# Down groups 1 to 3 of a hybrid block: three of four weight-block sums are accumulated in SBUF instead of in device memory

## The chip, the cores and the metric

The kernel runs on one core of one Trainium2 chip. The metric is the device time of one execution in microseconds (us); a kernel's time is the median of several runs. Where a profile is quoted it is one execution taken by the hardware profiler, with times counted from the start of its span.

## The reference

One layer of a hybrid block on 512 tokens of width 1024, all in float32: a gated delta rule branch and a retention branch, each gated and projected, added to the input after a norm, and then a feed-forward part. Only the last part bears on the change:

```python
hn = rmsnorm(x, n_mlp_pre)
ff = jnp.square(jax.nn.relu(hn @ w_up)) @ w_down      # 1024 -> 4096 -> 1024
return x + rmsnorm(ff, n_mlp_post)
```

## The kernel before, in words

**Feed-forward.** The 4096 hidden features are worked in four groups of 1024 (`for grp in range(4)`, L1991). In each group `feature_major` multiplies with `w_up`, the square of the relu is taken, and `seven_down` (L1885) multiplies 512 tokens x 1024 features with the 1024 x 1024 block of `w_down` that belongs to the group. That block is cut into quarters of 512 x 512, written 11, 12, 21, 22, and the product is made of seven products of quarters instead of eight (a Strassen-Winograd scheme). Three take a plain quarter of the weights (11, 12, and the one called s4, which is 22 of the columns); four take a sum of quarters. In the order of the code for groups 1 to 3: products 11, 12, s2, s1, s3, s4, 22. Group 4 (`grp == 3`) takes another order and is not touched.

**Weights.** Every quarter arrives in two halves of 128 partitions x 1024 numbers (512 KB). Each half is loaded by SyncE's queue into a `raw` tile, then split for TensorE into a rounded part `whi` (ScalarE, L148) and a rest `wlo` (VectorE, L149). `whi` and `wlo` have three buffers each, `raw` has two in each of two pools. TensorE then makes 12 matmuls with each half, 24 with each quarter (`token_product`, L303 to L325, L317).

**Block sums.** `BlockSums` (L155) makes the four sums of quarters in device memory while earlier stages run: it copies a quarter to a tensor `sums` (`copy`, L169, SyncE's queue) and adds further quarters or sums to it by accumulating transfers (`add_block`, L135, GpSimd's queue). `summed` then loads the halves as any other weight (`raw`, L183, L197). Of the four tensors of a group, `t[2]` holds 12+22, `t[1]` 11+12+22, `t[3]` all four, `t[0]` 11+12.

**Order.** A job (one half to copy or to add) is handed out in `pace` (L113), which every weight load calls: when the planned TensorE time `spent` has passed `queued`, one job is placed behind that load, and `queued` moves on by `JOB_US` = 8.5 us (L29, L121). Jobs not yet handed out when a sum is loaded are all issued at that point (L184 to L187). The order of instructions on each engine is fixed when the program is built, from program order, priorities (`tc.high_priority`) and which buffers come free; an engine issues in that order, and SyncE and GpSimd issue transfers in order too: one that waits holds all behind it.

**Tile `ym`.** The pool `pm` has four buffers of 128 x 1024 numbers under the tag `ym`; before the change they hold `fw` (L1773 and L1959), the weighted rows of the norms around the feed-forward part.

Of the kernel before, what the change touches and what calls it, by code (L numbers as in the profile page):

```python
# [19 lines left out]
P = 128  # L20
# [5 lines left out]
OFF_BA = 6144  # L26
OFF_QB, OFF_KB, OFF_VB, OFF_GB = 6160, 7184, 8208, 10256
OFF_GA, OFF_GBR = 12304, 13328
JOBS_FROM, JOB_US = 70.0, 8.5  # L29
SMALL_US, CONV_US, TOK_US, PK_US, INV_US, DB_US = 10.5, 6.5, 2.5, 2.0, 46, 1.2  # L30
VT_US, KS_US, PX_US, PC_US, GATE_US, FEAT_US, INV_PRIO, CONV_PRIO, SMALL_PRIO, KEY_PRIO, DECAY_US, AHEAD, TR_US, REC_PRIO, OUT_PRIO, SUM_PRIO = 2.5, 2.4, 3.5, 2.4, 11.0, 1.0, 0, 600, 800, 600, 20.0, 700, 2.2, 900, 900, 300
DFF = 4096
# [31 lines left out]
def hybrid_block_kernel(ctx: ExitStack, tc: tile.TileContext, a: dict, out: bass.AP):  # L64
# [68 lines left out]
    def add_block():  # L133
        dst, src, _ = later_adds.pop(0)
        tc.keep_in_program_order(nc.gpsimd.dma_start(dst, src, accum_op=ALU.add))  # L135
# [19 lines left out]
    class BlockSums:  # L155


        def __init__(self, src, c1, c2, tag, full=True):
            def block(kh, c):
                return src[4 * kh * P : 4 * (kh + 1) * P, c : c + 512].rearrange("(k p) c -> p k c", p=P)  # L160

            self.w12, self.first = block(0, c2), [block(0, c1), block(0, c1), block(1, c2), block(1, c1)]
            self.made = (2, 1, 3, 0) if full else (2, 0)
            self.t = {i: dr.tile([P, 4, 512], F32, tag=f"{tag}{i}", name="sums", bufs=1) for i in self.made}
            self.parts = []
            trickle.extend((self, i, k) for i in self.made for k in (0, 2))
# [13 lines left out]
        def weights(self, i, ks):  # L180
            return split_weights(self.raw(i, ks), 1024, 2)

        def raw(self, i, ks):  # L183
            while any(job[0] is self for job in trickle):  # L184
                copy_block()
            while any(dst is t for dst, *_ in later_adds for t in self.parts):
                add_block()  # L187
            return block_raw(self.t[i - 1][:, 2 * ks : 2 * ks + 2, :])

        def first_raw(self, i, ks):  # L190
            return block_raw(self.first[i][:, 2 * ks : 2 * ks + 2, :])

    def block_raw(block):
        n = next(loads)
        pool, tag = raw_pools[n % len(raw_pools)]
        raw = pool.tile([P, 1024], F32, tag=tag, name="raw", bufs=2)
        load = nc.sync.dma_start(raw.rearrange("p (k c) -> p k c", k=2), block)  # L197
        pace(load)
        return raw

    z_sums = BlockSums(w_in, OFF_ZA + 1024, OFF_ZA + 1536, "z")
    ga_sums = BlockSums(w_in, OFF_GA, OFF_GA + 512, "ga", False)
    vg_sums = [BlockSums(w_in, OFF_VB + h * 512, OFF_GB + h * 512, f"vg{h}", False) for h in range(4)]
    gb_sums = BlockSums(w_in, OFF_GBR, OFF_GBR + 512, "gb", False)
    down_sums = [BlockSums(w_down[grp * D : (grp + 1) * D, :], 0, 512, f"dn{grp}") for grp in range(4)]
    for sums in [z_sums, ga_sums] + vg_sums + [gb_sums] + down_sums:
        later_adds.extend((*pair, sums) for pair in sums.adds())

# [19 lines left out]
    def bank(pool):  # L228
        if pool is psx:
            return [psx.tile([P, T], F32, tag="dl", name="dl", bufs=3) for _ in range(2)]  # L230
        return [psm.tile([P, T], F32, tag="mm", name="mm") for _ in range(2)]

    def block_products(src, sums, product):


        def plain(pss, x, kh, c, first):
            for ks in range(2):
                product(pss, x, ks, weights(src, 4 * kh + 2 * ks, 2, c, 512, paced=False), first)

        def summed(pss, x, i, first):  # L240
            for ks in range(2):
                product(pss, x, ks, sums.weights(i, ks), first)

        return plain, summed
# [414 lines left out]
    class Clock:  # L659
# [36 lines left out]
        def ready(self, wait):  # L696
            if isinstance(wait, str):
                return self.events.get(wait, float("inf"))
            return wait
# [1018 lines left out]
    with tc.tile_pool(name="pm", bufs=1) as pm:  # L1718
# [165 lines left out]

        def seven_down(grp, x):  # L1885

            src = w_down[grp * D : (grp + 1) * D, :]
            plain, summed = block_products(src, down_sums[grp], token_product(x))

            def add(th, ch, parts, op=ALU.add, new=False, prio=400):  # L1890
                with tc.high_priority(prio):
                    for t in range(2):
                        dst = facc[:, 2 * th + t, hss[ch]]
                        if not new or grp:
                            nc.vector.tensor_tensor(dst, dst, parts[t], op)
                        elif op is ALU.add:
                            nc.scalar.copy(dst, parts[t])
                        else:
                            nc.scalar.mul(dst, parts[t], -1.0)

            a = bank(psx)
            plain(a, "11", 0, 0, True)
            add(0, 0, a, new=True, prio=100)
            b = bank(psm)
            plain(b, "12", 1, 0, True)
            add(0, 0, b, prio=0)
            c = bank(psm)

            def s1():
                summed(c, "s1", 1, True)  # L1910
                add(1, 1, c, new=True)

            def s2():
                summed(a, "s2", 2, False)
                add(0, 1, a, ALU.subtract, new=True)

            def s3():
                summed(a, "s3", 3, False)
                add(1, 1, a, ALU.subtract)

            for step in (s1, s2) if grp == 3 else (s2, s1, s3):
                step()
            plain(c, "s4", 1, 512, False)
            add(0, 1, c, prio=0)
            if grp < 3:
                summed(a, "22", 4, False)
                add(1, 0, a, new=True)
                return
            for t in range(2):
                rows = Finish(t)  # L1930
                for half in range(2):
                    rows.half(half)
                for half in range(2):
                    rows.store(half)
            ws = {}
            for name, i in (("s3", 3), ("22", 4)):
                kept = pm.tile([P, 8, T], F32R, tag=f"hn{i // 4}", name="keep").rearrange("p k t -> p (k t)")
                for ks in range(2):
                    hi, lo = (kept[:, 1024 * h : 1024 * h + 1024] for h in (2 * ks, 2 * ks + 1))
                    ws[name, ks] = split_weights(down_sums[3].raw(i, ks), 1024, 2, (hi, lo))  # L1940
            rows = [Finish(2 + t) for t in range(2)]
            for name, half, op in (("s3", 1, ALU.subtract), ("22", 0, ALU.add)):
                for t in range(2):
                    for ks in range(2):
                        token_product(x, (t,))(a, name, ks, ws[name, ks], False)
                    dst = facc[:, 2 + t, hss[half]]
                    with tc.high_priority(400):
                        done = nc.vector.tensor_tensor(dst, dst, a[t], op)
                    rows[t].half(half)
            for r in rows:  # L1950
                for half in range(2):
                    with tc.issue_after(done.ins):
                        r.store(half)
# [83 lines left out]
```

## Time and profile before

| what | us |
|---|---|
| median of 3 runs (1326.51 to 1328.75) | 1326.77 |
| the profiled execution, its own time | 1326.62 |
| its span | 1324.8 |
| TensorE busy (PE) | 1308.9 |
| VectorE busy (DVE) | 931.3 |
| ScalarE busy (ACT) | 668.7 |
| GpSimd busy (POOL) | 89.7 |

TensorE is busy in 99% of the span; the chain that ended last runs over PE for 89% of it. The 16 DMA engines moved 223.16 MB. GpSimd issues only the accumulating transfers and a few loads. In the profile, "wlo<-raw,whi" is the split on VectorE, "whi<-raw" that on ScalarE, "sums<-sums" a transfer between two sum tensors, and a mean duration of a matmul (0.39 us) is longer than the distance to the next one, since matmuls are pipelined.

### The profile page before, as it was taken

How to read it: one execution, taken by the hardware profiler on the slowest of the kernel's cores; microseconds unless marked ns; L12 is line 12 of the kernel's file. 1: busy time of each engine (PE TensorE's matmuls, PEld its weight loads, DVE VectorE, ACT ScalarE, POOL GpSimd, SP SyncE). 2: the span in 40 equal slices, each digit the busy share in tenths (PEclk: the TensorE clock that was granted, in tenths of full speed). 3: DMA queues.
4: the chain of work that ended last, by engine and by line, in shares of the span. 5: the costliest groups of instructions: out<-in, count | busy, mean ns of one | idle time of the engine just before them, and what ended most of it. 6: DMA issues, size and time to landing. Idle time of an engine off the chain costs nothing.

```text
span 1324.8 us, 17530 instructions
## 1 busy us (share of the span) xinstructions
PE 1308.9 (99%) x6591; PEld 1085.9 (82%) x6591; DVE 931.3 (70%) x1560; ACT 668.7 (50%) x1168; POOL 89.7 (7%) x95
## 2 busy tenths in 40 slices
PE   9999999999999999999999999999999999999997
PEld 7888787888888878888888888888889888888886
DVE  6889757486666578876567776789685746637478
ACT  5784546455534533544453443465266636355364
POOL 2100100000000001000010000000001000000001
PEclk9999999999999999999999999999999999999999
DMA  5336952476765568887293462545629895859635
GB/s 192 134 112 160 203 132 64 114 181 174 191 161 133 127 178 179 271 253 153 79 260 105 120 214 64 160 157 175 223 82 247 230 256 156 245 154 251 191 119 135
DMA packets 115557, 223.16 MB, mean 168 GB/s; under 512 B 6982, under 2 KB 38896, under 8 KB 114960
## 3 DMA queue, kind: packets, MB, share of 16 engines
q1 hardware_dynamic: 96496, 175.13, 41.3%
q0 software_dynamic: 16944, 40.54, 19.1%
q10 hardware_dynamic: 2032, 6.36, 1.3%
q8 instruction: 52, 0.85, 0.3%
q14 instruction: 33, 0.27, 0.1%
HBM read 216.75 MB, written 72.37 MB: 218 GB/s over the span
## 4 chain that ended last, share of the span: by engine, by line
PE 89%; DVE 6%; ACT 3%; issue 1%; DMA 1%; DVEq 0%; ACTq 0%
PE mm L668 18%; PE mm L317 17%; PE dl L317 11%; PE mm L93 10%; PE mm L95 10%; PE mm L94 10%; PE dl L668 5%; PE tr L397 1%; DVE wlo L149 1%; PE dl L94 1%; PE dl L95 1%; PE dl L93 1%; PE tr L677 1%; PE mm L632 1%; DVE tmp L1061 1%
## 5 line engine op out<-in xcount | busy, mean ns | idle before, releaser
L149 DVE TENSOR_TENSOR wlo<-raw,whi 128x1024 fp32r<-128x1024 f32 x269 | 328.2, 1222 | 204.2 <-ACT whi L148 203.1
L148 ACT CAST whi<-raw 128x1024 fp32r<-128x1024 f32 x269 | 282.6, 1052 | 356.5 <-PE mm L668 71.7
L668 PE MATMUL mm<-actT,whi 128*128 128x512 f32 x448 | 144.5, 403 | 0.0
L317 PE MATMUL mm<-whi,xsum 128*128 128x512 f32 x384 | 120.6, 390 | 0.0
L95 PE MATMUL mm<-hn,wlo 128*128 128x512 f32 (+1 forms) x288 | 105.4, 366 | 0.0
L94 PE MATMUL mm<-hn,whi 128*128 128x512 f32 (+1 forms) x288 | 105.3, 366 | 0.0
L93 PE MATMUL mm<-hn,whi 128*128 128x512 f32 (+1 forms) x288 | 105.3, 366 | 0.0
L668 PEld LDWEIGHTS mm<-actT,whi 128*128 128x128 f32 x448 | 80.6, 188 | 14.8
L668 PE MATMUL mm<-actT,wlo 128*128 128x512 f32 x224 | 87.7, 392 | 0.0
L317 PEld LDWEIGHTS mm<-whi,xsum 128*128 128x128 f32 x384 | 71.8, 188 | 14.9
L317 PE MATMUL mm<-wlo,xsum 128*128 128x512 f32 x192 | 74.8, 390 | 0.0
L317 PE MATMUL dl<-whi,ffq 128*128 128x512 f32 x224 | 71.3, 389 | 0.0
L668 PE MATMUL mm<-whi,og 128*128 128x512 f32 x192 | 62.3, 397 | 0.0
L95 PEld LDWEIGHTS mm<-hn,wlo 128*128 128x128 f32 x288 | 54.3, 189 | 8.8
L93 PEld LDWEIGHTS mm<-hn,whi 128*128 128x128 f32 x288 | 54.3, 189 | 8.7
L94 PEld LDWEIGHTS mm<-hn,whi 128*128 128x128 f32 x288 | 54.3, 189 | 8.7
L668 PE MATMUL mm<-whi,actT 128*128 128x512 f32 x176 | 60.3, 405 | 1.0 <-DVE qf L906 1.0
L317 PE MATMUL dl<-whi,actT 128*128 128x512 f32 x192 | 61.1, 390 | 0.0
L317 PE MATMUL mm<-whi,ffq 128*128 128x512 f32 x192 | 60.9, 389 | 0.0
L1830 DVE TENSOR_TENSOR ffq<-r,ffq 128x512 fp32r<-128x512 f32 (+1 forms) x64 | 39.2, 621 | 28.0 <-ACT ffq L1830 27.9
L135 POOL DMA_DIRECT2D sums<-in_w_in_dram x28 | 32.6, 1164 | 359.8 <-DMA sums<-in_w_in_dram 359.8
L93 PE MATMUL mm<-actT,whi 128*128 128x512 f32 x128 | 51.5, 402 | 0.0
(394 smaller groups left out, 2839.4 us busy)
## 6 DMA issues: line engine op xcount, KB each, us to landing
raw<-in_w_in_dram SPq DMA_DIRECT2D x95, 512.0 KB, 4.9
raw<-sums SPq DMA_DIRECT2D x64, 512.0 KB, 4.4
raw<-in_w_up_dram SPq DMA_DIRECT2D x36, 512.0 KB, 7.2
sums<-in_w_in_dram SPq DMA_DIRECT2D x32, 512.0 KB, 5.2
sums<-in_w_down_dram SPq DMA_DIRECT2D x32, 512.0 KB, 6.9
sums<-in_w_in_dram POOLq DMA_DIRECT2D x28, 512.0 KB, 7.4
raw<-in_w_down_dram SPq DMA_DIRECT2D x24, 512.0 KB, 5.9
sums<-sums POOLq DMA_DIRECT2D x20, 512.0 KB, 8.5
```

The costliest lines, as they stand in the source:

```text
L93: nc.tensor.matmul(ps, lh, rh, start=first, stop=False)
L94: nc.tensor.matmul(ps, lh, rl, start=False, stop=False)
L95: nc.tensor.matmul(ps, ll, rh, start=False, stop=last)
L135: tc.keep_in_program_order(nc.gpsimd.dma_start(dst, src, accum_op=ALU.add))
L148: nc.scalar.copy(hi[:, :n], raw[:, :n])
L149: nc.vector.tensor_tensor(lo[:, :n], raw[:, :n], hi[:, :n], ALU.subtract)
L317: m = nc.tensor.matmul(pss[t], lhs[i // 2], rhs[i % 2], start=first and k + i == 0, stop=k + i == 5, skip_group_check=not first,)
L397: nc.tensor.transpose(ps, src, ident)
L632: pin(nc.tensor.matmul(first_keys[f][:, 256:512], ws[w][:, kk, :], xs[x][:, 2 * j + kk, 256:512], start=False, stop=kk == 1 and i == 2, sk ...
L668: m = tc.keep_in_program_order(nc.tensor.matmul(*args, **kwargs))
L677: tc.keep_in_program_order(nc.tensor.transpose(ps, src, ident if by is None else by))
L1830: return nc.scalar.copy(dst[0], r), nc.vector.tensor_tensor(dst[1], r, dst[0], ALU.subtract)
```

## The change

For groups 1 to 3 only `t[2]` (12+22) is still made in device memory (`made=(2,)`). The other three sums are made in four tiles of tag `ym`:

- `u`, two tiles, one for each half: loaded with quarter 11, split for product 11, then `t[2]` is added to it by an accumulating transfer (12+22, giving 11+12+22), split for product s2, then quarter 21 is added (all four), split for product 22.
- `v`, two tiles: loaded with quarter 12, quarter 11 is added at once (11+12), split for product s1.

`s3` still loads `t[2]`; 12 and s4 load plain quarters as before. All accumulating transfers go through GpSimd's queue. `JOB_US` goes from 8.5 to 10.5.

The transfers in the program, each of 512 KB: copies to `sums` from `w_down` 32 before, 14 now; accumulating transfers for the down groups 32 before and 32 now, of which 18 now end in SBUF; loads from `sums` for down groups 32 before, 14 now; loads of quarters of `w_down` into `raw` 24 before, 18 now, and 12 more into `u` and `v`.

```diff
-JOBS_FROM, JOB_US = 70.0, 8.5
+JOBS_FROM, JOB_US = 70.0, 10.5
...
+        def grown(self, pool, tag):
+
+            def halves(w):
+                return [w[:, 2 * ks : 2 * ks + 2, :] for ks in range(2)]
+
+            def tiles(src):
+                return [block_raw(w, pool.tile([P, 1024], F32, tag=tag, name="sum", bufs=4)) for w in halves(src)]
+
+            def plus(raws, src):
+                for raw, w in zip(raws, halves(src)):
+                    nc.gpsimd.dma_start(raw.rearrange("p (k c) -> p k c", k=2), w, accum_op=ALU.add)
+
+            return tiles, plus
...
-    down_sums = [BlockSums(w_down[grp * D : (grp + 1) * D, :], 0, 512, f"dn{grp}") for grp in range(4)]
+    down_sums = [
+        BlockSums(w_down[grp * D : (grp + 1) * D, :], 0, 512, f"dn{grp}", (2,) if grp < 3 else (2, 1, 3, 0))
+        for grp in range(4)
+    ]
...
+            if grp < 3:
+                sums.ready()
+                u = tiles(sums.first[0])
+                v = tiles(sums.w12)
+                plus(v, sums.first[0])
             a = bank(psx)
-            plain(a, "11", 0, 0, True)
+            if grp < 3:
+                times(a, "11", u, True)
+                plus(u, sums.t[2])
+            else:
+                plain(a, "11", 0, 0, True)
...
             def s1():
-                summed(c, "s1", 1, True)
+                if grp < 3:
+                    times(c, "s1", v, True)
+                else:
+                    summed(c, "s1", 1, True)
...
             def s2():
-                summed(a, "s2", 2, False)
+                if grp < 3:
+                    times(a, "s2", u, False)
+                    plus(u, sums.first[3])
+                else:
+                    summed(a, "s2", 2, False)
...
             if grp < 3:
-                summed(a, "22", 4, False)
+                times(a, "22", u, False)
```

TensorE's order and form of instructions are the same in both programs, and so are VectorE's and ScalarE's, apart from the tiles' names. What moves stands on the two queues.

GpSimd's queue from the first group's last accumulate to the second group's (before: all into `sums`; after: `sum_9012` and `sum_9014` are `u` of the first group, `sum_9016` and `sum_9018` its `v`). Before:

```order
L1723 DMA post_8590<-in_norm_mlp_post_dram 128x1024
L135 DMA sums_95<-in_w_down_dram 128x2x512
L135 DMA sums_96<-sums_95 128x1024
L135 DMA sums_97<-sums_96 128x1024
L135 DMA sums_98<-in_w_down_dram 128x2x512 x2
L135 DMA sums_99<-in_w_down_dram 128x2x512
L135 DMA sums_100<-sums_99 128x1024
```

The same place after the change:

```order
L1744 DMA post_8566<-in_norm_mlp_post_dram 128x1024
L135 DMA sums_93<-in_w_down_dram 128x2x512
L206 DMA sum_9016<-in_w_down_dram 128x2x512
L206 DMA sum_9018<-in_w_down_dram 128x2x512
L206 DMA sum_9012<-sums_91 128x1024
L206 DMA sum_9014<-sums_91 128x1024
L206 DMA sum_9012<-in_w_down_dram 128x2x512
L206 DMA sum_9014<-in_w_down_dram 128x2x512
L135 DMA sums_93<-in_w_down_dram 128x2x512
L135 DMA sums_94<-in_w_down_dram 128x2x512
```

The six accumulates of the group now stand in one row, two for `v` and four for `u`, each of `u` behind the split that reads the old contents.

SyncE's queue where the first group's down product ends and the second group's `w_up` loads begin. Before:

```order
L197 DMA raw_9215<-sums_91 128x1024
L103 DMA raw_9235<-in_w_down_dram 128x2x512
L103 DMA raw_9253<-in_w_down_dram 128x2x512
L169 DMA sums_101<-in_w_down_dram 128x2x512
L197 DMA raw_9274<-sums_93 128x1024
L197 DMA raw_9292<-sums_93 128x1024
L103 DMA raw_9322<-in_w_up_dram 128x2x512
L103 DMA raw_9352<-in_w_up_dram 128x2x512
L103 DMA raw_9383<-in_w_up_dram 128x2x512
```

The same place after (`sum_9599` and `sum_9602` are `u` of the second group, `sum_9604` and `sum_9606` its `v`):

```order
L215 DMA raw_9192<-sums_91 128x1024
L103 DMA raw_9212<-in_w_down_dram 128x2x512
L169 DMA sums_96<-in_w_down_dram 128x2x512
L103 DMA raw_9231<-in_w_down_dram 128x2x512
L215 DMA sum_9599<-in_w_down_dram 128x2x512
L215 DMA sum_9602<-in_w_down_dram 128x2x512
L103 DMA raw_9295<-in_w_up_dram 128x2x512
L169 DMA sums_97<-in_w_down_dram 128x2x512
L103 DMA raw_9326<-in_w_up_dram 128x2x512
L103 DMA raw_9356<-in_w_up_dram 128x2x512
L169 DMA sums_97<-in_w_down_dram 128x2x512
L103 DMA raw_9387<-in_w_up_dram 128x2x512
```

The two loads of product 22 are gone, and the next group's `u` loads stand ahead of the first `w_up` load.

VectorE's order from product 11's second half to product s2's second half, in the third group, before:

```order
L149 TENSOR_TENSOR wlo_10266<-raw_10263,whi_10265 128x1024
L1830 TENSOR_TENSOR ffq_9906<-r4_9903,ffq_9906 128x2x256
L1872 TENSOR_TENSOR r4_9903<-r4_9903 128x512
L149 TENSOR_TENSOR wlo_10285<-raw_10281,whi_10284 128x1024
L1873 TENSOR_TENSOR r4_9903<-r4_9903 128x512
L1895 TENSOR_TENSOR facc_8592<-facc_8592,dl_10220 128x512
L1874 TENSOR_TENSOR r4_9903<-r4_9903 128x512
L149 TENSOR_TENSOR wlo_10310<-raw_10307,whi_10309 128x1024
```

After:

```order
L149 TENSOR_TENSOR wlo_10240<-raw_10237,whi_10239 128x1024
L1851 TENSOR_TENSOR ffq_9875<-r4_9872,ffq_9875 128x2x256
L1893 TENSOR_TENSOR r4_9872<-r4_9872 128x512
L149 TENSOR_TENSOR wlo_10258<-raw_10255,whi_10257 128x1024
L1894 TENSOR_TENSOR r4_9872<-r4_9872 128x512
L1922 TENSOR_TENSOR facc_8568<-facc_8568,dl_10197 128x512
L1895 TENSOR_TENSOR r4_9872<-r4_9872 128x512
L149 TENSOR_TENSOR wlo_10278<-sum_10187,whi_10277 128x1024
```

Nothing moved; the last row, product s2's first half, now reads the grown tile.

## Rows read from the trace of the kernel before

**Rows 1.** The page, part 1: busy us, share of the span, instructions.
```profile
span 1324.8 us, 17530 instructions
...
PE 1308.9 (99%) x6591; PEld 1085.9 (82%) x6591; DVE 931.3 (70%) x1560; ACT 668.7 (50%) x1168; POOL 89.7 (7%) x95
```

**Rows 2.** Waits of TensorE: engine, line, waited for: us, times, longest.
```profile
PE warm L475 <- DVE warm L464: 1.2, 1, 1.2
PE mm L668 <- DVE qf L906: 1.0, 1, 1.0
...
PE dl L94 <- DVE wlo L149: 0.4, 1, 0.4
...
PE tr L677 <- ACT vt L909: 0.2, 1, 0.2
```

**Rows 3.** Timeline of TensorE, first down group: start, us, line, tiles.
```profile
1033.86 0.39 PE L317 MATMUL dl<-whi,ffq 128*128 128x512 f32 x1
...
1044.74 0.39 PE L317 MATMUL dl<-whi,ffq 128*128 128x512 f32 x1
1044.96 0.39 PE L317 MATMUL dl<-wlo,ffq 128*128 128x512 f32 x1
...
1047.68 0.39 PE L317 MATMUL dl<-wlo,ffq 128*128 128x512 f32 x1
...
1071.94 0.39 PE L93 MATMUL mm<-hn,whi 128*128 128x512 f32 x1
```

**Rows 4.** Timeline of VectorE, first down group.
```profile
1024.04 1.23 DVE L149 TENSOR_TENSOR wlo<-raw,whi 128x1024 fp32r<-128x1024 f32 x1 [0.94 <-ACT whi L148]
...
1029.77 1.22 DVE L149 TENSOR_TENSOR wlo<-raw,whi 128x1024 fp32r<-128x1024 f32 x1
...
1041.00 1.22 DVE L149 TENSOR_TENSOR wlo<-raw,whi 128x1024 fp32r<-128x1024 f32 x1
...
1043.94 1.22 DVE L149 TENSOR_TENSOR wlo<-raw,whi 128x1024 fp32r<-128x1024 f32 x1
...
1048.79 1.23 DVE L149 TENSOR_TENSOR wlo<-raw,whi 128x1024 fp32r<-128x1024 f32 x1 [0.69 <-ACT whi L148]
...
1065.06 1.22 DVE L149 TENSOR_TENSOR wlo<-raw,whi 128x1024 fp32r<-128x1024 f32 x1 [1.49 <-ACT whi L148]
```

**Rows 5.** Timeline of ScalarE, first down group.
```profile
1042.21 1.06 ACT L148 CAST whi<-raw 128x1024 fp32r<-128x1024 f32 x1
...
1047.70 1.05 ACT L148 CAST whi<-raw 128x1024 fp32r<-128x1024 f32 x1 [1.67 <-PE dl L317]
...
1068.97 1.05 ACT L148 CAST whi<-raw 128x1024 fp32r<-128x1024 f32 x1 [3.94 <-DMA raw<-in_w_up_dram]
```

**Rows 6.** The page, part 6: transfer, queue, count, KB each, median us to landing.
```profile
raw<-sums SPq DMA_DIRECT2D x64, 512.0 KB, 4.4
raw<-in_w_up_dram SPq DMA_DIRECT2D x36, 512.0 KB, 7.2
...
sums<-sums POOLq DMA_DIRECT2D x20, 512.0 KB, 8.5
```

**Rows 7.** Landing of L135's accumulates: 1025 to 1300 us (15 of them), then 1000 to 1020.
```profile
DMA to landing us min/median/max: 7.7/9.8/13.1
...
DMA to landing us min/median/max: 9.1/14.6/21.7
```

**Rows 8.** Timeline of SyncE's queue at the end of the first down group.
```profile
1058.63 5.33 SPq L103 DMA_DIRECT2D raw<-in_w_up_dram  x3
```

**Rows 9.** Timeline of SyncE's queue and of GpSimd, the first block sums.
```profile
295.26 0.34 SPq L197 DMA_DIRECT2D raw<-sums  x1
...
171.39 1.14 POOL L135 DMA_DIRECT2D sums<-in_w_in_dram  x1 [13.90 <-DMA sums<-in_w_in_dram]
```

More of the change, by code (lines that the diff above doesn't have):

```diff
@@ L155, in hybrid_block_kernel, with __init__ @@
     class BlockSums:
-        def __init__(self, src, c1, c2, tag, full=True):
+        def __init__(self, src, c1, c2, tag, made=(2, 1, 3, 0)):
             def block(kh, c):
@@ L162, in __init__ @@
             self.w12, self.first = block(0, c2), [block(0, c1), block(0, c1), block(1, c2), block(1, c1)]
-            self.made = (2, 1, 3, 0) if full else (2, 0)
+            self.made = made
             self.t = {i: dr.tile([P, 4, 512], F32, tag=f"{tag}{i}", name="sums", bufs=1) for i in self.made}
@@ L181, in weights, with ready @@
             return split_weights(self.raw(i, ks), 1024, 2)
-        def raw(self, i, ks):
+        def ready(self):
             while any(job[0] is self for job in trickle):
@@ L187, in raw @@
                 add_block()
+        def raw(self, i, ks):
+            self.ready()
             return block_raw(self.t[i - 1][:, 2 * ks : 2 * ks + 2, :])
@@ L191, in first_raw, with block_raw @@
             return block_raw(self.first[i][:, 2 * ks : 2 * ks + 2, :])
-    def block_raw(block):
+        def grown(self, pool, tag):
[7 more added lines that the diff above has]
+            return tiles, plus
+    def block_raw(block, raw=None):
         n = next(loads)
         pool, tag = raw_pools[n % len(raw_pools)]
-        raw = pool.tile([P, 1024], F32, tag=tag, name="raw", bufs=2)
+        if raw is None:
+            raw = pool.tile([P, 1024], F32, tag=tag, name="raw", bufs=2)
         load = nc.sync.dma_start(raw.rearrange("p (k c) -> p k c", k=2), block)
@@ L201, in hybrid_block_kernel @@
     z_sums = BlockSums(w_in, OFF_ZA + 1024, OFF_ZA + 1536, "z")
-    ga_sums = BlockSums(w_in, OFF_GA, OFF_GA + 512, "ga", False)
-    vg_sums = [BlockSums(w_in, OFF_VB + h * 512, OFF_GB + h * 512, f"vg{h}", False) for h in range(4)]
-    gb_sums = BlockSums(w_in, OFF_GBR, OFF_GBR + 512, "gb", False)
-    down_sums = [BlockSums(w_down[grp * D : (grp + 1) * D, :], 0, 512, f"dn{grp}") for grp in range(4)]
+    ga_sums = BlockSums(w_in, OFF_GA, OFF_GA + 512, "ga", (2, 0))
+    vg_sums = [BlockSums(w_in, OFF_VB + h * 512, OFF_GB + h * 512, f"vg{h}", (2, 0)) for h in range(4)]
+    gb_sums = BlockSums(w_in, OFF_GBR, OFF_GBR + 512, "gb", (2, 0))
+    down_sums = [
+        BlockSums(w_down[grp * D : (grp + 1) * D, :], 0, 512, f"dn{grp}", (2,) if grp < 3 else (2, 1, 3, 0))
+        for grp in range(4)
+    ]
     for sums in [z_sums, ga_sums] + vg_sums + [gb_sums] + down_sums:
@@ L1885, in seven_down, with times @@
         def seven_down(grp, x):
-            src = w_down[grp * D : (grp + 1) * D, :]
-            plain, summed = block_products(src, down_sums[grp], token_product(x))
+            src, sums = w_down[grp * D : (grp + 1) * D, :], down_sums[grp]
+            product = token_product(x)
+            plain, summed = block_products(src, sums, product)
+            tiles, plus = sums.grown(pm, "ym")
+            def times(pss, name, raws, first):
+                for ks in range(2):
+                    product(pss, name, ks, split_weights(raws[ks], 1024, 2), first)
             def add(th, ch, parts, op=ALU.add, new=False, prio=400):
```

## The prediction

> **What bounds the kernel now.** I read the page's busy times first. TensorE is busy for 1308.9 of the 1324.8 us of the span [rows 1], so a gain can only come out of the 15.9 us in which it isn't, or out of its own work. The change leaves its own work alone: the orders show TensorE with the same instructions in the same order and forms. So I read next the list of its waits, over the whole span [rows 2]. It has 16 rows that add up to 7.7 us. The reader is to see that the largest is 1.2 us and that a single row names a split of weights as what was waited for: 0.4 us, once, "dl <- DVE wlo". The same list for 1000 to 1325 us alone, in which all four down groups lie, has no row at all. The rest of the idle time, 15.9 − 7.7 = 8.2, is the start, the end, and gaps too small to be listed. TensorE therefore waits for no weights in the stretch that is changed, and removing transfers there can give back nothing. In the whole span at most the 0.4 us is theirs.
>
> Then I read the timelines of the first down group on three engines, for how far ahead of TensorE the weights are, because the change lengthens the road of some of them.
>
> **The road that grows.** TensorE starts product 11 at 1033.86, s2 at 1044.74, and the second half of s2 needs its `wlo` at 1047.68; the group ends and the next begins at 1071.94 [rows 3]. VectorE splits the two halves of 11 long before that, 1024.04 + 1.23 = 1025.27 and 1029.77 + 1.22 = 1030.99; the halves of s2 are split at 1041.00 and 1043.94 [rows 4]. Before, each half of s2 had its own load, which waited only for a `raw` buffer. After, it must go: the last read of `u` by the split of 11, an accumulating transfer of 512 KB, cast, split, TensorE. A cast and a split together take from 1047.70, when a cast starts, to 1048.79 + 1.23 = 1050.02: 2.32 us [rows 4, 5]. So for the second half, which has the shorter time:
>
> - the accumulate can be issued at 1030.99 (0.06 added for the semaphore, an estimate: 1031.05);
> - the cast must start by 1047.68 − 2.32 = 1045.36;
> - so the transfer may take up to 14.3 us before TensorE waits, and up to 1042.21 − 1031.05 = 11.2 before even the cast starts later than it did [rows 5].
>
> For the first half the same arithmetic gives 1044.96 − 2.32 − 1025.33 = 17.3 us, and it is first in the queue. Both halves may overlap; their splits are 5.7 us apart.
>
> No row of the kernel before shows an accumulate whose end is in SBUF. The bounds from below are a plain load from `sums` of the same size, 4.4 us, and from above the accumulates into device memory: median 8.5 for sum onto sum in the page [rows 6], and over 1025 to 1300 us, 15 of them in the same traffic, 7.7 to 13.1 with a median of 9.8 [rows 7]. The farthest row is 21.7, between 1000 and 1020 us, where three were issued in a row and shared the engines [rows 7]. I take 8.5, since the operation nearest to the new one (a contiguous tensor added to another, 512 KB) has that. At 4.4, 8.5 and 13.1 the cost to TensorE is 0, because what hides it is product 11 and product 12 ahead of s2, 10.9 us of matmuls [rows 3]. Only at 21.7 does it show: (21.7 − 14.3) × 3 groups = 22 us.
>
> The Trainium skill ("DMA: Bandwidth & Descriptors", section "Anatomy of one DMA — SWDGE (gpsimd) path") gives a fit for one transfer issued from GpSimd, about 2.0 us plus the bytes over 436 GB/s; for 512 KB that makes an estimate of 3.2 us. By it the margin would be four times what is needed. The trace doesn't agree for accumulates, which took 7.7 to 13.1 [rows 7], and the rows decide; the sum is 0 either way.
>
> **The other new roads.** `v`'s accumulate (11 onto 12) waits only for its load, and s1 follows s2, so it has more time than `u`. The second growth (21 onto `u`) can go when s2's splits end, 1042.22 and 1045.16, and product 22's second split was at 1065.06 [rows 4]; less the cast there are some 18 us for it. Cost 0 for both up to 13.1 us of transfer.
>
> **What waits on the queues.** GpSimd's accumulates for `u` now each wait for a split, and hold what is behind them: the block sums of later groups. Those are needed a group later, 80 us on, and take some 10 us each [rows 7]. Cost 0. On SyncE's queue the next group's `u` loads now stand ahead of the first `w_up` load. They wait for the tiles that `v` had, which s1's splits let go at 1050.02 [rows 4]. The first `w_up` load was issued only at 1058.63 [rows 8]; it waited for `raw` buffers that s1, s4 and 22 no longer ask for as often. It should now go earlier by some microseconds, and ScalarE's wait of 3.94 us for it at 1068.97 [rows 5] should shrink or go. That is worth nothing on the clock: TensorE had no wait there at 1071.94.
>
> **The wider spacing.** Jobs 10.5 instead of 8.5 us apart move the early sums later by a factor of 1.24 from 70 us on. The tightest is the first: its last accumulate was issued at 171.39 and its first load at 295.26 [rows 9]. With 7 us of landing, 70 + (178.4 − 70) × 1.24 = 204, still 91 us ahead. Fewer and rarer transfers could also ease other loads. Bounds: −0.4 (the one wait on a split goes) to +1.2 (a new wait as long as the longest there is [rows 2]); I take 0, as the lead is some 90 us.
>
> **Sum.** The profiled execution took 1326.62 us, 1324.8 of span and 1.8 around it. TensorE's work 0, `u` 0, `v` 0, queues 0, spacing 0: 1326.6. That is 0.15 below the median of 1326.77, the scatter of the three runs being 1326.51 to 1328.75. A change of 0.2% (2.7 us) is about what a measurement of this kernel can tell from none, so "same" is 1324.1 to 1329.4.
>
> **Rivals.**
>
> *u's second half lands late (slower).* Place: before s2's second half in each of the three groups, with "dl <- DVE wlo" as TensorE's wait. It decides from a transfer of 14.3 us. At 16 us it costs 1.7 × 3 = 5, giving about 1332; at 21.7 it costs 22, giving about 1349. For it: accumulates issued close together reached 21.7 [rows 7], and now `v`'s two and `u`'s two may share GpSimd's queue and the engines at that point, beside plain loads. Against: all 15 in this stretch stayed at 13.1 or less, and `v`'s two don't wait for 11's splits, so they should be gone by then. Chance 0.08.
>
> *The next group's `u` holds SyncE's queue (slower).* If its tiles came free only with the split of product 22 (1065.06 + 1.22 = 1066.28 [rows 4]), the first `w_up` load behind it would land at 1066.28 + 7.2 [rows 6], be cast and split by 1075.8, and TensorE, due at 1071.94, would stand for 3.8 us at two changes of group: 7.7, giving 1334. For it: the order on the queue is exactly that. Against: the tiles it waits for are `v`'s. Chance 0.02.
>
> *The early sums come late.* With 91 us of lead, and of the size of the 1.2 above if it happens through contention: 1327.8, inside "same" anyway; as a real delay, over 1329.4, chance 0.01.
>
> *Faster.* Fewer transfers (18 copies to `sums` and 18 loads from it go, 6 plain loads come) would have to take away waits of TensorE. Behind weights there are 0.4 us, giving 1326.2; even all 7.7 of the list would give 1318.9, but the other rows name vector results that no transfer feeds. What speaks for it is only that the 8.2 us outside the list might hold something. Chance of more than 0.2%: 0.03.
>
> *The change doesn't do what it says.* If the accumulates were so slow or so late that the growth ran one after the other, it is the first rival again; the program does build the sums in the same number of accumulates, so nothing else is left out.
>
> **How the numbers follow.** No change has 0.86; with it goes its own range of 1326.2 (the 0.4 gone) to 1327.8 (the 1.2 added). The slower ones have 0.08 + 0.02 + 0.01 = 0.11, faster 0.03. The range that holds 8 in 10 has to take in the scatter of the runs, up to 1328.75, and a little of each side: 1325.2 to 1329.0. It doesn't reach the late landing, which is left out with the other rivals, 0.14 in all.
>
> **What would show it.** Right: TensorE's list of waits for 1000 us to the end stays empty; accumulates into `u` land in under 14.3 us, and ScalarE, if it waits for them, starts the second cast of s2 no later than 11.5 us after TensorE's start of product 11; the `w_up` loads of groups 2 and 3 are issued earlier than 1058.63, and ScalarE's 3.94 us wait is smaller; TensorE's busy time is again about 1309. Wrong: rows "dl <- DVE wlo" near 1047, 1129 and 1210 us (slow landing), or "mm <- DVE wlo" near 1072 and 1153 (the held queue), or new waits on `raw<-sums` before 1000 us (the spacing). A gain of over 2.7 us would say that TensorE lost time to transfers in a way its list of waits doesn't show.

## The result, and the profile after

The changed kernel is slower: 1330.36 us median of 11 runs (1329.31 to 1336.55) against 1327.48 of 11 (1326.51 to 1328.75), a ratio of 1.0027 with a 95% interval of 1.0016 to 1.0039. Run again in a second series it was 1.0030 (1.0019 to 1.0041). By these ratios some 3.6 to 4 us are lost (the medians of the two series lie 2.9 and 5.3 us apart), where 0 was forecast.

The page after, its span and its part 1, as in [rows 1]:

```profile
span 1327.7 us, 17485 instructions
...
PE 1309.3 (99%) x6591; PEld 1085.5 (82%) x6591; DVE 931.9 (70%) x1560; ACT 669.3 (50%) x1168; POOL 92.6 (7%) x95
```

TensorE's work is the same within 0.4 us; of the 2.9 us by which this execution's span is longer, 2.5 are idle time. TensorE's waits after, from 300 us to the end (waited for: us, times, longest), show no split of weights:

```profile
PE mm L93 <- ACT r L1846: 1.1, 1, 1.1
PE dl L689 <- ACT vt L1395: 0.6, 1, 0.6
PE tr L698 <- DVE vt L1428: 0.4, 1, 0.4
PE dl L93 <- ACT osq L1637: 0.3, 1, 0.3
PE tr L418 <- DVE fw L1828: 0.3, 1, 0.3
```

Three of them wait for a result of ScalarE, `r`, `vt` of L1395 and `osq`, and have no counterpart in the list of before, from which [rows 2] are taken. When they come is read by laying the same instructions of both traces side by side. TensorE before, around the start of the feed-forward part:

```profile
997.86 0.41 PE L397 MATMUL tr<-cmat,fw 128*128 128x128 f32 x2 [0.29 <-DVE fw L1807]
...
1012.07 0.40 PE L93 MATMUL mm<-hn,whi 128*128 128x512 f32 x1
```

The same two after, and then the starts of product 11, of the first `wlo` of s2's second half, and of the second group:

```profile
999.45 0.41 PE L418 MATMUL tr<-cmat,fw 128*128 128x128 f32 x2 [0.29 <-DVE fw L1828]
...
1014.97 0.50 PE L93 MATMUL mm<-hn,whi 128*128 128x512 f32 x1 [1.15 <-ACT r L1846]
...
1036.86 0.39 PE L338 MATMUL dl<-whi,ffq 128*128 128x512 f32 x1
...
1050.69 0.39 PE L338 MATMUL dl<-wlo,ffq 128*128 128x512 f32 x1
...
1074.94 0.39 PE L93 MATMUL mm<-hn,whi 128*128 128x512 f32 x1
```

TensorE is 1.59 us late at 999 us, 2.90 late at 1015, 3.00 late where product 11 begins, and still 3.00 (3.01 at s2) at the next group [rows 3]. From 1016 us to the end its list of waits is empty, as before. So all is lost ahead of the down groups: about 1.6 us in small pieces before 999 us, and 1.3 between 999 and 1015.

The largest of the small pieces is the wait on `vt` near 344 us. ScalarE's rows there show a cast that waits for a load, and `vt` behind it:

```profile
343.75 1.06 ACT L148 CAST whi<-raw 128x1024 fp32r<-128x1024 f32 x1 [2.66 <-DMA raw<-in_w_in_dram]
344.71 0.83 ACT L1395 ACTIVATE vt<-dl,eg 128x256 f32<-128x256 f32 x2
```

What holds TensorE between 999 and 1015 us is read from the chain that ended last (start, us, what), the kernel after:

```profile
1001.24 12.24 DMA raw<-in_w_up_dram
...
1013.59 1.05 ACT whi L148
1014.63 0.29 ACT r L1846
...
1014.97 0.50 PE mm L93
```

This load, the sixth of the eight `w_up` loads that are issued from 984 to 1010 us, takes 12.24 us. In before the sixth is issued at 999.5 us, and its row reads

```profile
DMA to landing us min/median/max: 9.1/9.1/9.1
```

so it lands at 1008.6, only 0.7 us ahead of its cast at 1009.27, which waits for TensorE and not for the load. After, the cast waits for the load. It stands on ScalarE ahead of `r`, which TensorE needs: ScalarE takes its instructions in their order, so a late load holds up results that have nothing to do with weights. SyncE's queue after shows what stands among those loads:

```profile
985.84 2.67 SPq L103 DMA_DIRECT2D raw<-in_w_up_dram  x3
988.56 4.05 SPq L215 DMA_DIRECT2D sum<-in_w_down_dram  x3
994.64 3.18 SPq L103 DMA_DIRECT2D raw<-in_w_up_dram  x2
997.87 1.45 SPq L2051 DMA_DIRECT2D out_dram<-acc  x1
1000.78 0.37 SPq L215 DMA_DIRECT2D sum<-in_w_down_dram  x1
1001.24 6.91 SPq L103 DMA_DIRECT2D raw<-in_w_up_dram  x3
```

These are the four first loads of `u` and `v` of the first group, 2 MB, which go as soon as the `ym` buffers are free. Over 1000 to 1010 and 1010 to 1020 us the DMA engines are busy throughout in both kernels (share 1.05 and 1.07 after, 1.01 and 1.03 before, by the windows view); after, they move more in that time (334 and 292 GB/s against 248 and 231).

### The profile page after: what moved, and what is told of

Read it like the earlier page. It is cut to its first block, busy times and chain, and to the rows that moved or that the text cites. A ratio compares the mean times of both kernels' runs of the same rounds, so it can differ in the third digit from the quotient of the medians.

```text
span 1327.7 us, 17485 instructions
## 1 busy us (share of the span) xinstructions
PE 1309.3 (99%) x6591; PEld 1085.5 (82%) x6591; DVE 931.9 (70%) x1560; ACT 669.3 (50%) x1168; POOL 92.6 (7%) x95
## 4 chain that ended last, share of the span: by engine, by line
PE 84%; DVE 7%; ACT 5%; DMA 2%; issue 1%; DVEq 0%; ACTq 0%
PE mm L689 16%; PE mm L338 16%; PE dl L338 10%; PE mm L93 10%; PE mm L95 10%; PE mm L94 10%; PE dl L689 5%; DVE wlo L149 2%; PE dl L93 1%; PE dl L95 1%; PE dl L94 1%; PE tr L418 1%; PE tr L698 1%; DMA raw<-sums 1%; DMA raw<-in_w_up_dram 1%
## 5 line engine op out<-in xcount | busy, mean ns | idle before, releaser
L149 DVE TENSOR_TENSOR wlo<-raw,whi 128x1024 fp32r<-128x1024 f32 x245 | 299.5, 1224 | 207.7 <-ACT whi L148 207.0
L148 ACT CAST whi<-raw 128x1024 fp32r<-128x1024 f32 x245 | 257.8, 1053 | 351.9 <-PE mm L338 74.1
L135 POOL DMA_DIRECT2D sums<-in_w_in_dram x28 | 32.6, 1164 | 479.9 <-DMA sums<-in_w_in_dram 479.9
L93 PEld LDWEIGHTS mm<-hn,whi 128*128 128x128 f32 x288 | 54.3, 189 | 10.1 <-ACT r L1846 1.4
```

Of the source, the lines that this page charges most:

```text
L93: nc.tensor.matmul(ps, lh, rh, start=first, stop=False)
L148: nc.scalar.copy(hi[:, :n], raw[:, :n])
L149: nc.vector.tensor_tensor(lo[:, :n], raw[:, :n], hi[:, :n], ALU.subtract)
```

## The experiments

Each kernel ran 4 to 12 times beside before on the same chip; a ratio is to that, with its 95% interval. The expectations name theories. Of the whole loss: A, the spacing costs 1.6 us and the first group's loads 1.3; B, all is the new tiles and loads; C, all is the spacing. Then D, the loads among `w_up` and the spacing are all of it; E, the jobs that are gone cost something of their own; F, the down groups cost nothing and transfers in new places before 1016 us all; G, the down groups cost it; H, the transfers of jobs that the shorter list puts beside other loads.

**What chance does.** `f3_before_again` is before, unchanged.

> The kernel before, unchanged: its ratio to itself says how far such a ratio is from 1 by chance (0.1% expected), and a second trace says which places differ from one execution to the next without any change (some tenths of a us at a few places expected; 1 us or more at one place would say that the places in a single trace prove little).

0.9994 (0.9986 to 1.0003). Its trace differs from the first by up to 0.75 us at single places (0.55 less near 497 us, 0.75 more near 582), and TensorE ends 0.1 us later. A ratio within 0.1% proves nothing, and a place is only used below if several traces or a ratio bear it out.

**The two parts apart.** `e1_spacing`: before with

```diff
-JOBS_FROM, JOB_US = 70.0, 8.5
+JOBS_FROM, JOB_US = 70.0, 10.5
```

> The kernel before with the jobs 10.5 instead of 8.5 us apart, nothing else. Aligned instruction by instruction, TensorE after the change is 1.7 us later by the end of the branches (about 998 us), 1.3 us more between 998 and 1015, and nothing more until the end. Theory A, two costs: the spacing makes the first part, so this kernel takes about 1.6 us more than before (1329) and its TensorE is on time again relative to that in the feed-forward part. Theory B, all comes from the new tiles and loads of the first down group: no change, 1327.5. Theory C, the spacing alone makes all of it by moving jobs into the start of the feed-forward part: 3 us more, 1330.4, with a wait of ScalarE on w_up loads near 1001.

1.0001 (0.9993 to 1.0010): with the old list of jobs the spacing costs nothing that can be told. `e2_grown` is the changed kernel with 8.5.

> The changed kernel with the jobs 8.5 us apart as before: the sums grown in SBUF alone. Theory A: only the 1.3 us between 998 and 1015 are lost, 1328.8. Theory B: all 3 us stay, 1330.4. Theory C: none, 1327.5. The down groups from 1015 on: TensorE waits for nothing, accumulates of a sum tensor into the tiles u land in 5 to 7 us, under the bound of 14.3.

1.0019 (1.0007 to 1.0030): the rest of the change costs it. Its trace, of the slowest of its twelve runs, has no wait of TensorE over 0.3 us after 985 us, though the four loads stand among `w_up` as in the changed kernel: the same sixth `w_up` load takes 10.1 us there, and its cast waits 2.37 us, but TensorE doesn't. Between 300 and 985 us TensorE waits 2.4 us on `osq`, and 1.4 and 0.8 on splits: theory A named the wrong place for it.

**The four loads.** `e6_before_loads` adds to before, in the first group, nothing but

```diff
+            if grp == 0:
+                for k in range(4):
+                    extra = pm.tile([P, 1024], F32, tag="ym", name="sum", bufs=4)
+                    block = w_down[(2 * k) * P : (2 * k + 2) * P, 0:512].rearrange("(k p) c -> p k c", p=P)
+                    nc.sync.dma_start(extra.rearrange("p (k c) -> p k c", k=2), block)
```

> The kernel before with nothing changed but four more loads of 512 KB from w_down into four tiles ym that nobody reads, which stand on SyncE's queue among the first w_up loads at the same places as u and v of the first group in the changed kernel; all sums are made as before. Theory D: these loads alone make w_up land late, ScalarE waits for it 2 to 6 us near 1001 to 1014, TensorE then waits for ScalarE's r, and the time is 1.5 to 2.5 us over before. Theory E: no change from before, since the grown sums aren't there.

1.0028 (1.0016 to 1.0040), as much as the whole change. TensorE's wait over 985 to 1020 us, and then the windows (us, busy time and instructions of each engine, granted clock, DMA share, GB/s) of this kernel:

```profile
PE mm L93 <- ACT r L1825: 2.2, 1, 2.2
```

```profile
1000.00:1010.00 10.00, 9.71 (x83) 9.54 (x82) 5.72 (x7) 6.74 (x14) 0.86 (x1) 1.00 1.04 307
1010.00:1020.00 10.00, 7.83 (x52) 7.11 (x52) 3.66 (x5) 4.53 (x10) 4.30 (x4) 0.94 1.04 296
1020.00:1030.00 10.00, 10.00 (x41) 8.13 (x41) 3.82 (x5) 4.69 (x11) 0.00 (x0) 0.89 1.08 244
```

The wait is the one of the changed kernel, at twice the length, and the granted clock falls behind it: after 2.2 us without work TensorE ran for a part of these stretches at 1.2 instead of 2.4 GHz (41 matmuls of 512 columns in the last 10 us, against 46 at 1.00 in the same stretch of the changed kernel). The changed kernel's own wait of 1.15 us left its clock at 1.00 in its trace. Beside before, TensorE falls 4.1 us behind at this place; another 2.5 us of this execution are lost near 582 us, ahead of the four loads, on splits (1.8 us of waits).

`e3_loads_behind` is the changed kernel with these four loads behind the group's last `w_up` load (`latest[0]`, kept in `weights`); `f4_loads_behind_again` is the same.

```diff
+                with ExitStack() as behind:
+                    if grp == 0:
+                        behind.enter_context(tc.issue_after(latest[0].ins))
-                u = tiles(sums.first[0])
-                v = tiles(sums.w12)
+                    u = tiles(sums.first[0])
+                    v = tiles(sums.w12)
```

> The changed kernel, with the four loads of u and v of the first down group issued behind the last w_up load of that group instead of among them. Theory A: the w_up loads near 1001 land in about 5 to 7 us instead of 12, ScalarE's wait for them goes, TensorE's 1.15 us wait near 1014 goes, and the time is 1.3 us less than the changed kernel's: about 1329. Theory C: unchanged at 1330.4. If u now comes late for product 11, TensorE waits for a split near 1035 instead.

> The kernel of e3_loads_behind again, for a second trace and its time beside f1 and f2. Theory F: 1 to 2 us over before, because the jobs at 10.5 us and those that are gone put others beside the loads between 550 and 800 us; no wait of ScalarE for w_up between 985 and 1016.

1.0011 (1.0002 to 1.0021) and 1.0020 (1.0006 to 1.0034). In both traces the wait on `r` is gone (from 985 us on, only 0.3 us on `fw` is left, which before has too), and product 11 still gets `u` in time. Part of the loss stays. In the trace of `e3_loads_behind` a piece of it, 0.9 us, comes near 685 us, where TensorE waits 0.6 us on `osq` behind this cast:

```profile
685.02 1.05 ACT L151 CAST whi<-raw 128x1024 fp32r<-128x1024 f32 x1 [4.63 <-DMA raw<-in_w_in_dram]
```

`e4_groups_2_3` makes the first group as before, to have no `u` and `v` at its start.

> The changed kernel with the first down group made as before (all four sums in device memory, no u and v), groups 2 and 3 grown, spacing 10.5. Theory A: no u and v loads at the start of the feed-forward part, so the 1.3 us near 1001 to 1014 go, about 1329; but the first group's sums are then made later than before, with three times the jobs left. Theory B: about 1327.5 to 1328. Theory C: 1330.4 or more.

1.0043 (1.0027 to 1.0058), against all three theories. The four loads are still there, at 988 and 1000 us: they are now the second group's, which move up into the free buffers. The wait on `r` is 3.0 us. And at 10.5 us the first group's sums are not done in time, so accumulates are issued in a row beside them. It shows the collision once more, and not what it was made for.

`f2_before_loads_behind` is `e6_before_loads` with the loads behind `w_up`.

> The kernel before with the same four extra loads as in e6_before_loads, now behind the last w_up load of the first group instead of among them. Theory F: where they stand decides, not that they are there: the time is that of before within 0.7 us, against 3.7 us over it in e6_before_loads. Otherwise (the extra 2 MB themselves cost it): again 2.5 us or more.

1.0070 (1.0057 to 1.0083): worse, against the expectation. Here nobody reads the extra loads, and they stand ahead of the quarter that product 11 does read; TensorE waits 3.7 us for its casts and splits after 1016 us. In `e3_loads_behind` the same four loads are that quarter and the next. In both places that were tried, 2 MB ahead of weights that are due cost something.

**The list of jobs.** `e5_behind_85` is `e3_loads_behind` with 8.5.

> The changed kernel with the four loads of the first group's u and v behind its last w_up load, as in e3_loads_behind, and the jobs 8.5 us apart as before. Theory D, the whole loss is the collision of these loads with the w_up loads (about 2 us) and the spacing (about 0.6 us): both are out, so the time is that of before within 0.5 us. Theory E, the jobs that are gone from the list move others and this costs something more of its own: 1 us or more above before. TensorE has no wait of 0.5 us or more from 985 us to the end.

1.0034 (1.0023 to 1.0044): theory D falls. The loss lies at one place. TensorE's wait over 560 to 990 us, the landing of the two loads of weights issued between 766 and 771 (before: 5.2 to 6.3 us over 762 to 772), ScalarE's cast of one of them, and the windows:

```profile
PE dl L93 <- ACT osq L1640: 2.2, 1, 2.2
```

```profile
DMA to landing us min/median/max: 11.7/11.7/11.7
```

```profile
778.56 1.05 ACT L151 CAST whi<-raw 128x1024 fp32r<-128x1024 f32 x1 [5.09 <-DMA raw<-in_w_in_dram]
```

```profile
770.00:780.00 10.00, 10.00 (x45) 8.00 (x43) 5.34 (x8) 4.59 (x6) 1.18 (x2) 1.00 1.04 253
780.00:790.00 10.00, 7.81 (x28) 6.25 (x28) 5.33 (x17) 5.18 (x13) 1.14 (x1) 0.83 0.95 244
```

It is the same chain as at 1001 us: late load, cast that waits 5.09 us, `osq` behind it on ScalarE, a gap of 2.2 us, and a lower clock after it. In before SyncE's copies stand among these loads too, at 763.55 and 769.04 us. What is new beside the load is on GpSimd's queue, which from 750 to 780 us has one accumulate in before,

```profile
771.32 0.81 POOL L135 DMA_DIRECT2D sums<-sums  x1 [24.58 <-DVE p L298]
```

and three in `e5_behind_85`:

```profile
759.78 0.85 POOL L138 DMA_DIRECT2D sums<-sums  x1 [12.17 <-DMA sums<-in_w_down_dram]
769.20 0.81 POOL L138 DMA_DIRECT2D sums<-sums  x1 [8.56 <-DMA sums<-in_w_down_dram]
774.07 1.17 POOL L138 DMA_DIRECT2D sums<-in_w_down_dram  x1 [4.06 <-DMA sums<-in_w_down_dram]
```

Three kernels ask what makes the load late. `f1_jobs_kept` has the grown sums, the loads behind `w_up`, and all jobs of before:

```diff
-        BlockSums(w_down[grp * D : (grp + 1) * D, :], 0, 512, f"dn{grp}", (2,) if grp < 3 else (2, 1, 3, 0))
+        BlockSums(w_down[grp * D : (grp + 1) * D, :], 0, 512, f"dn{grp}")
```

> The sums of groups 1 to 3 grown in SBUF as in the changed kernel, but with every job of before still handed out at 8.5 us (the sums that nobody loads are made in device memory as well), and the four first loads of u and v behind the first group's last w_up load. SyncE's, GpSimd's and the other queues are those of before up to about 1006 us, so this is the grown sums in the down groups alone. Theory F: these cost nothing, as the prediction has it, and the loss comes from transfers that stand elsewhere before 1016 us: the time is that of before within 0.7 us. Theory G: the down groups cost it: 2 us or more over before.

1.0002 (0.9993 to 1.0011). The grown sums in the down groups cost nothing that can be told. `g2_list_alone` is the reverse, before with the short list alone (`made=(2,)` for groups 1 to 3, and `raw` loads `self.first[i - 1]` where there is no sum).

> The kernel before with its 8.5 us, where for groups 1 to 3 only the sum 12+22 is made and the other sums' products load a plain quarter of w_down instead (another result, the time is of interest): the short list of jobs of the changed kernel without u, v or any accumulate in SBUF. Theory H: the list alone costs it, as in e5_behind_85: 3 to 5 us over before, with the wait on osq near 780. Otherwise, if the list costs only together with grown sums: within 0.7 us of before.

1.0032 (1.0018 to 1.0045): at 8.5 us the list alone costs as much as the change does. TensorE's wait in its trace (of the slowest of its eight runs), 560 to 990 us, and the stretch around it:

```profile
PE dl L93 <- ACT osq L1617: 2.9, 1, 2.9
```

```profile
780.00:790.00 10.00, 7.13 (x25) 5.48 (x24) 3.91 (x7) 4.67 (x11) 0.00 (x0) 0.80 1.02 260
```

Beside before, TensorE falls 6.0 us behind here, and 3.2 near 497 us, where it waits 1.4 us on a split.

`g1_no_jobs_780` is `e5_behind_85` with no job at that place. `REST` is a stretch of planned time in which no job is handed out; it begins later here, so that the jobs pushed back still find room ahead of it:

```diff
+        if 745.0 < queued[0] < 790.0:
+            queued[0] = 790.0
-REST = 860.0, 985.0
+REST = 905.0, 985.0
```

> The kernel of e5_behind_85 (4.5 us over before; its trace has a 2.2 us wait of TensorE on ACT osq near 780 and a granted clock of 0.83 behind it) with no job handed out between 745 and 790 us of planned time; the two copies and the accumulates of that stretch come behind it. Theory H, these transfers delay the load of weights whose cast holds ScalarE: the wait near 780 goes and the granted clock stays at 1.00 there, the time falls by some 3.5 us to 1328 to 1329, unless the moved jobs meet the next such place near 875. If the wait stays, the transfers of jobs are not what delays the load.

1.0001 (0.9992 to 1.0009): 0.33% are back. In its trace the copies at 764.81 and 769.48 us and the accumulates at 774.07 and 786.62 us of `e5_behind_85` are gone from this place, and the jobs behind them come later; accumulates at 762.16 and 771.21 us remain, and the four loads of `w_in` there land in 6.3 to 9.1 us. The list of waits for 560 to 990 us is empty, and the windows read

```profile
770.00:780.00 10.00, 10.00 (x46) 8.29 (x45) 8.87 (x12) 5.89 (x9) 0.81 (x1) 1.00 1.02 284
780.00:790.00 10.00, 10.00 (x46) 8.29 (x45) 4.55 (x16) 5.61 (x13) 0.00 (x0) 1.00 0.28 106
```

`g3_placeholders` is `f1_jobs_kept` where the jobs of sums that nobody loads keep their place but issue nothing.

> The kernel of f1_jobs_kept, where the jobs of sums that nobody loads keep their place in the list but issue no transfer: grown sums, loads of u and v behind w_up, the remaining jobs where they stood before, 18 copies and 14 to 18 accumulates fewer. Theory H: no transfer is in a new place, so the time is that of before or, if the missing transfers free a load that was late, up to 0.7 us less: 1326.5 to 1327.8; no wait on osq. If it is 1.5 us or more over before, places alone are not the cause.

0.9995 (0.9986 to 1.0004). Growing the sums with no transfer in a new place is as fast as before, and no faster: the 18 copies and the loads that it saves were hidden. No version beat before. `f1_jobs_kept` and `g3_placeholders` have neither the four loads among `w_up` nor a job in a new place, and both are at the time of before: with these two out, nothing of the loss is left.

**The bound of 14.3 us.** `e7_late_landing` is `e3_loads_behind` with three accumulates in place of one:

```diff
-                plus(u, sums.t[2])
+                for _ in range(3):
+                    plus(u, sums.t[2])
```

> The kernel of e3_loads_behind with three accumulates instead of one onto each half of u between product 11 and product s2 (12+22 added three times: another result, the time is of interest). They follow each other, so the last lands some 17 to 22 us after the split of 11 instead of 5 to 6. By the prediction's bound of 14.3 us TensorE must now wait before s2 in each of the three groups, for 3 to 8 us each and 10 to 24 in all, more if its granted clock falls after the wait: 1340 to 1353. If the bound is wrong and there is more cover than that, the time stays at e3_loads_behind's 1329.3.

1367.48 us, 1.0300 (1.0283 to 1.0316). TensorE's waits from 1016 us on:

```profile
PE dl L341 <- ACT whi L151: 21.6, 6, 5.1
PE dl L341 <- DVE wlo L152: 3.7, 6, 0.8
```

They fall before the two halves of s2 in each of three groups, as the bound says. The road was longer than I expected, since each accumulate waited for the one ahead: in the first group the cast could start at 1059.52 and the split of 11 had ended at 1033.55; less the prediction's 0.06 that is a road of 25.9 us. Less 14.3 that is 11.6, or 35 if it is the same in all three groups, and so the time is beyond the 1353 expected; measured were 1367.5 − 1329.3 = 38.1, of which 25.3 are the waits. The rest fits the granted clock behind them: 0.87 over 1050 to 1090 us takes about 0.13 x 40 = 5.2 us, and the later groups show 0.87 over 40 us and 0.93 over 50. The runs thus bear out a bound somewhere between the 5 to 7 us at which nothing waited and 25.9; 14.3 itself was not approached from both sides.

**The changed kernel again**, `e8_changed_again`.

> The changed kernel again, for its time beside the others on one chip and for a second trace of it. Theory D: 2.5 to 3.5 us over before, ScalarE waits for w_up between 998 and 1015 again, and no wait of TensorE from 1016 us to the end. The places of the other 1.7 us in the first trace (344, 591, 686 us) were of that execution and need not come back; theory E would have them come back at the same places.

1.0030 (1.0019 to 1.0041). In this trace the wait on `r` is only 0.4 us, and other pieces stand at 159, 569, 591, 686 and 771 us: two of five (591 and 686) are those of the first trace. Those at 569 and 771 are waits on splits, 1.1 us together. How much is lost where differs from one execution to the next; the ratio does not.

## Why the prediction was wrong

The step that failed is the term "queues 0", and with it "spacing 0": the loads and jobs that the change puts in new places were followed only at the changes of group and only to their own readers. In place of 0 the runs showed 3.6 to 4 us, lost ahead of the down groups.

**Right.** TensorE's own work (0), the accumulates into `u` and `v` (0), and the queues at the change of group. The unknown price came out nearer its lower end: the first group's accumulates of `t[2]` into `u` took, from issue to landing,

```profile
DMA to landing us min/median/max: 5.4/5.4/5.5
```

where 8.5 was taken between 4.4 and 13.1. They were issued 0.3 us after the split, where 0.06 was put. All twelve accumulates into `u` took 5.4 to 6.6 us. The six into `v` took 9.0 to 20.6, the longest beyond the 13.1 up to which the prediction worked out its 0; none made TensorE wait. The estimate of 3.2 from the Trainium skill ("DMA: Bandwidth & Descriptors", "Anatomy of one DMA — SWDGE (gpsimd) path") was too low for an accumulate here as well. The bound of 14.3 fits `e7_late_landing`. SyncE's queue after the first group's product and ScalarE's casts there:

```profile
1056.20 0.37 SPq L103 DMA_DIRECT2D raw<-in_w_up_dram  x1
```

```profile
1072.42 1.06 ACT L148 CAST whi<-raw 128x1024 fp32r<-128x1024 f32 x1 [1.66 <-PE dl L338]
```

The first `w_up` load goes 1056.20 − 3.00 = 1053.2 by the old clock, 5.4 us earlier than in [rows 8]; the wait of 3.94 us in [rows 5] is gone, and TensorE gained nothing by it, all as forecast.

**Wrong, first: "TensorE therefore waits for no weights".** For what the change takes away the sentence holds: transfers dropped without moving others gave nothing back (`g3_placeholders`). But I also took the rows that name a split (0.4 us) as all that late weights can cost, and wrote that the other rows "name vector results that no transfer feeds". That is a misreading of the list: four of its rows name ScalarE, as `vt` in [rows 2], and one a transfer. Casts of weights share ScalarE's order with `vt`, `osq` and `r`, and the loads that landed late near 344, 685, 778 and 1013 us showed as waits on those. Waits on `osq` of 0.2 to 2.9 us are in all eight traces whose list is the short one of groups 1 to 3 (after, `e2`, `e3`, `e5`, `e7`, `e8`, `f4`, `g2`), and in none of before, `f3`, `e1`, `e6`, `f1`, `f2`, `g3`, nor in `e4`, whose list is short in two groups only, nor in `g1`, which has the short list without the jobs near 780 us.

**Wrong, second: what the wider spacing and the shorter list move.** The term "spacing 0" asked only whether a sum would be late for its reader. I never asked beside which loads the moved transfers would come to stand. A new wait was allowed for, as the +1.2 under the spacing and in the rival of 1327.8, but its size was that of the longest wait in before's list, the one on `warm`, and was not worked out from what the moved transfers meet. The spacing alone was 0 (`e1_spacing`); the term that I left out is the list, shortened by 18 copies and 18 accumulates, whose remaining jobs move: 0.32 to 0.34% at 8.5 us (`g2_list_alone`, `e5_behind_85`), and 0.11 to 0.20% at 10.5 (`e3`, `f4`).

**Wrong, third: the queue was followed at the wrong place.** The order of SyncE's queue was read at the changes of group, where `u` loads meet `w_up` loads with time to spare. At the first group's start the same loads meet `w_up` loads of which the sixth had 0.7 us to spare in before; added to before alone they cost 0.28% (`e6_before_loads`). A load of weights took longer where other transfers stood beside it: 12.24 us against 9.1 for the sixth `w_up` load, and 11.7 against 6.3 for the `w_in` load near 767 us beside copies and accumulates. The page "DMA: Bandwidth & Descriptors" of the Trainium skill, section "Issuing engines are not separate DMA queues", says that transfers of all issuing engines run on the same 16 DMA engines and interleave. These rows agree with it.

The prediction's sign of being right, an empty list of TensorE's waits from 1000 us on, failed by one row, the 1.1 us on `r`. Its signs of being wrong pointed elsewhere: TensorE has no wait on a split near 1047, 1129 or 1210 us or at the changes of group. ScalarE's waits on `raw<-sums` before 1000 us did grow, from 0.5 to 8.4 us in all, but they were 6.4 in `e1_spacing`, which lost nothing.

**What stays open.** How the changed kernel's 0.27 to 0.30% divides: 0.07 to 0.19 go with the four loads (`e3` and `f4` against it) and 0.11 to 0.20 are left to the list at 10.5 us, but the intervals overlap. At 8.5 us `e2_grown` lost less with the loads among `w_up` (0.19%) than `e5_behind_85` with them behind (0.34%); their intervals overlap, but the trace of `e2` shows no wait on `r`, so what the four loads cost may depend on where the jobs stand. That the sixth `w_up` load is later because of the four loads is shown by `e6`. Which of the transfers near 780 us delay the `w_in` load was not taken apart: the copies are there in before, and two of the accumulates are there in `g1`, and in neither is the load late, so it may take both.

## What to carry to other kernels

Where an engine that casts or splits weights also makes results for TensorE, late weights need not show as waits on weights: look also for waits on that engine's other results, and for the loads ahead of them in its order. For any change that drops, adds or respaces background transfers, list what stands beside each load that is due soon, before and after, at every place that moves and not only where the new code is. And keep the remaining transfers where they stood when others are dropped; the places were worth 0.3% here, the dropped transfers nothing.

## What the runs showed of the hardware

A gap of 2 to 3 us in TensorE's work cost up to twice its length and more, but not always. Laid beside before, TensorE fell 4.1 us behind at the gap of 2.2 us in `e5_behind_85` (granted clock 0.83 over the 10 us around it), 4.1 at the 2.2 of `e6_before_loads` (0.94 and 0.89), and 6.0 at the 2.9 of `g2_list_alone` (0.80, then 0.86). In `g1_no_jobs_780`, without the gap, the same place has 1.00. But the gap of 3.0 us in `e4_groups_2_3` cost 3.3, and the clock stayed at 1.00 in the windows around it and behind it:

```profile
1010.00:1020.00 10.00, 7.03 (x44) 6.16 (x43) 2.27 (x4) 4.48 (x11) 7.93 (x7) 1.00 1.09 269
1020.00:1030.00 10.00, 10.00 (x46) 8.29 (x45) 3.71 (x5) 4.82 (x10) 0.00 (x0) 1.00 1.10 252
```

So the length of a gap alone doesn't say here whether the clock falls; what else decides it stays open. In `f4_loads_behind_again` TensorE stood 2.2 us near 159 us with no engine or transfer shown as the cause ("issue"), and in `e8_changed_again` 0.6 us; both have jobs at 10.5 us, and what they waited for stays open.
